# Turning half of a residual stream on TensorE instead of by VectorE and strip transfers, and spreading the strips that remain

## The chip, the core and the metric

The kernel runs on one core of a Trainium2 chip. It is a single launch; the metric is the device time of that launch in microseconds (us). The engines are TensorE (PE), VectorE (DVE), ScalarE (ACT), GpSimd (POOL) and SyncE (SP). In this kernel SP issues nearly all transfers, one after the other from one queue.

## What is computed

A trunk of two layers works on x of 256 rows and 2048 columns (float32), with 256 memory rows beside it. Each layer computes

```
h = rmsnorm(x, norm_g[l]);  proj = h @ w_in[l]              # 2048 x 7168
y_a = B * conv3(C * x_A) * silu(g_A)                        # 6 groups of 128 channels
y_d = headnorm(softmax(q1 k1) v - lam * softmax(q2 k2) v) * silu(g_D)   # 6 heads, q and k normed, distance bias
mkv = rmsnorm(mem, mem_norm_g[l]) @ w_mem_kv[l]             # 2048 x 1024
mk, mv = mkv[:, :512], mkv[:, 512:]                         # mk is normed per head of 128
y_m = softmax(mq mk) mv * silu(g_M)                         # 4 heads
x = x + concat(y_a, y_d, y_m) @ w_out[l]                    # 2048 x 2048
```

The memory keys mk and values mv of both layers depend on `mem` alone. The queries of the memory heads, and so the first use of mk, come late in a layer.

## The kernel before

**Blocks and chunks.** Every product with a weight matrix is cut into blocks of 512 output columns (`block`, line 264). A block has two accumulators (256 rows are two times 128) and goes over the 16 tiles of 128 rows of the weight. Two such tiles are a chunk: one load of 512 KB into `raw` (L249, four buffers), then ACT rounds it to `hi` and DVE takes the rest as `lo` (L259 and L260 with a gain for the memory weights, L255 and L256 for the others; four buffers each). Float32 is thus made of two rounded parts, and PE does three products for each of two row tiles and two weight tiles: `hi`, `lo` and once more `hi` against the stationary operand's two parts (L280 to L282). That is 12 matmuls of 128x512 per chunk and 8 chunks per block.

**Order of the work.** First the memory keys and values: layer 0's keys (chunks 0 to 7), layer 0's values (8 to 15), layer 1's keys (16 to 23), layer 1's values (24 to 31). Their stationary operand is `memT`, the transposed memory. From chunk 32 on layer 0 begins, whose first six blocks (32 to 79) give the queries, keys, values and a gate of the differential attention; the stationary operand is `xT`, x transposed and scaled by `norm_g`, as a pair of rounded parts. Then come the blocks of the memory heads' queries and gate, those of the convolution, and the output product, whose stationary operand is `yT`. Layer 1 does the same.

**Two ways of transposing.** One is on PE: `rows_T` (L568) has PE transpose tiles of 128x128 into PSUM, four of them (two column tiles by two row tiles) into one of two `pt` buffers, and ACT and DVE split the result into `xT` (`split_T`, L238 and L239, or L235 and L236 without a gain). `x_rows` (L577) does so for a list of column tiles, one group of four per step. The other way leaves PE alone: `turn_sheet` (L379) has DVE transpose the 32x32 blocks of a quarter, 512 columns by 256 rows, into a "sheet" (L386 from x, L383 in place), and then 16 transfers between parts of SBUF, called strips (L396, 32 KB each for a full sheet), move the blocks to their places. `x_turned` (L582) does so for a quarter of x, then splits it two column tiles at a time. The queries and keys of each layer, the memory keys and queries, and the operands of the convolution go by strips too.

**Planner.** After each chunk of a block the function `run_side` (L195) is called: it counts the chunk, issues up to `at_once[0]` strips from a queue `shifts`, steps every job in `tasks` whose due chunk has come, and steps one job in `side`. `later(job, n)` makes a job due n chunks from now. A job from `turn_sheet` first has DVE do its transposes, waits four or five chunks, puts its 16 strips into the queue and goes on when the last has been issued. `at_once` is 7 until layer 0's first block is done and 5 from then on. The strips stand on SP between the weight loads; while SP issues one it issues nothing else.

**The work that the change touches.** During layer 1's key block `x_load` (L644) loads x, two column tiles (256 KB) per chunk, into the buffer `xs`, which held `mem` before. After every second such load a quarter of x is complete, and an `x_turned` job is put into `tasks`: four quarters, with the buffers `v`, `ga`, `mga` and `mqT`, which are free until layer 0 needs them under those names. All 64 strips go into `shifts`. The memory keys are normed (`normed`, L341) into a sheet and turned by the job `keys` (L639), layer 0's from chunk 19 on, layer 1's from chunk 36 on; both sheets come from the two buffers of `e`, which the sheets of x use too (L585, L637, L663). At the end ACT scales them (L642).

The program's instructions are put into an order for each engine ahead of time; those marked by `keep_in_program_order`, the strips among them, stay in the order of the program among themselves. A queue or engine then works through its list strictly in order.

Of the kernel before, what the change touches and what calls it, by code (L numbers as in the profile page):

```python
# [18 lines left out]
P = 128  # L19
# [4 lines left out]
KT = D_MODEL // P  # L24
# [8 lines left out]
NB = 512  # L33
# [12 lines left out]
def encoder(ctx: ExitStack, tc: tile.TileContext, x, mem, norm_g, w_in, conv_w, conv_b,  # L46
# [20 lines left out]
    def nm(s):  # L67
        uid[0] += 1
        return f"{s}_{uid[0]}"
# [52 lines left out]
    def g_norm(l, k):  # L122
        return cvb[:, 64 + l * KT + k:65 + l * KT + k]
# [33 lines left out]
    def rsqrt(t, n):  # L157

        y = small.tile([P, n], F32, tag=f"rs_y{n}", name=nm("rsy"))
        a = small.tile([P, n], F32, tag=f"rs_a{n}", name=nm("rsa"))  # L160
        yi = y.bitcast(I32)
        nc.vector.tensor_scalar(yi, t.bitcast(I32), 1, None, ALU.logical_shift_right)
        nc.vector.tensor_scalar(yi, yi, -1.0, float(0x5F3759DF), ALU.mult, ALU.add)
        for _ in range(3):
            nc.vector.scalar_tensor_tensor(a, y, -0.5, y, ALU.mult, ALU.mult)
            nc.vector.tensor_tensor(a, a, t, ALU.mult)
            nc.vector.scalar_tensor_tensor(y, a, 1.5, y, ALU.add, ALU.mult)
        return y
# [2 lines left out]


    side, tasks, shifts = deque(), [], deque()
    at_once = [7]
    due = {}
    chunk = [0]

    def later(g, n):
        due[id(g)] = chunk[0] + n
        return g  # L180
# [157 lines left out]
    def col(st, which, t):  # L338
        return st[:, which, t:t + 1]

    def normed(acc, gs, st, home):  # L341

        ng = NB // gs
        ss = small.tile([P, NT, ng], F32, tag=f"ss{ng}", name=nm("ss"))
        for t in range(NT):
            sq = tmp.tile([P, NB], F32, tag="nat", name=nm("sq"), bufs=4)
            nc.scalar.activation(sq, acc[t], AF.Square)
            nc.vector.tensor_reduce(ss[:, t], sq.rearrange("p (g d) -> p g d", d=gs), AX.X, ALU.add)
            nc.vector.tensor_scalar(ss[:, t], ss[:, t], col(st, R2_64 if gs == HALF else R2_128, t), EPS,
                                    ALU.mult, ALU.add)  # L350
        r = rsqrt(ss.rearrange("p t g -> p (t g)"), NT * ng).rearrange("p (t g) -> p t g", t=NT)
        both = home()
        for t in range(NT):
            nc.vector.tensor_scalar(r[:, t], r[:, t], col(st, R, t), None, ALU.mult)
            w = min(gs // B, NA)
            nc.vector.tensor_tensor(
                both[:, :, :, t].rearrange("p (g b) j c -> p j g b c", b=w),
                acc[t].rearrange("p (j g b c) -> p j g b c", g=NA // w, b=w, c=B),
                r[:, t].rearrange("p (j g) -> p j g", g=NA // w).unsqueeze(3).unsqueeze(4)
                .to_broadcast([P, NB // P, NA // w, w, B]), ALU.mult)  # L360
        return both
# [4 lines left out]
    def sheet(home, tag, n=NB // P):  # L366
        return home.tile([P, NA, n, NT, B], F32, tag=tag, name=nm("sh"))

    def sheets(tag):
        return lambda: sheet(tmp if tag == "e" else keep, tag)  # L370
# [197 lines left out]
    def rows_T(dst, src, k, gain=None, n=2):  # L568

        pt = ps_t.tile([P, 2, SEQ], F32, tag="t", name=nm("pt"))  # L570
        for j in range(n):
            for t in range(NT):
                nc.tensor.transpose(pt[:, j, t * P:(t + 1) * P], src(k + j, t), ident)  # L573
        for j in range(n):
            split_T(dst, k + j, pt[:, j, :], None if gain is None else gain(k + j))

    def x_rows(dst, l, ks):  # L577
        for k in ks:
            rows_T(dst, lambda k, t: xs[:, t, k * P:(k + 1) * P], k, lambda k: g_norm(l, k))
            yield  # L580

    def x_turned(dst, l, b, tag, **how):  # L582

        whole = keep.tile([P, NB // P, SEQ], F32, tag=tag, name=nm("xf"))
        yield from turn_sheet(whole, sheet(tmp, "e"),  # L585
                              of=xs[:, :, b * NB:(b + 1) * NB], **how)
        for j in range(NB // P):
            k = b * NB // P + j
            pinned[0] = True
            split_T(dst, k, whole[:, j], g_norm(l, k))  # L590
            pinned[0] = False
            if j % 2:
                yield

    def stats_of(parts, tag):
        ss = small.tile([P, NT], F32, tag="ssum", name=nm("ssum"))
        nc.vector.tensor_reduce(ss, parts, AX.X, ALU.add)
        return row_stats(ss, tag)

    def T_tile(what):  # L600
        kept.append(big.tile([P, 2, KT, SEQ], F32R, tag="T", name=nm(what)))
        return kept[-1]
# [20 lines left out]
    def mem_square(k):  # L623

        load_constants((1, 2, 0, None)[k // 2] if k < 8 else None)
        if k == 8:
            rest_of_constants()
        if k < 8:
            c = k // 2
            for t in range(NT):  # L630
                sq = tmp.tile([P, NB], F32, tag="nat", name=nm("sq"), bufs=4)
                tc.keep_in_program_order(
                    nc.scalar.activation(sq, xs[:, t, c * NB:(c + 1) * NB], AF.Square, accum_out=ssm[:, t, c:c + 1]))

        if k == 10:
            stm.append(stats_of(ssm, "stm"))
            tasks.append(later(keys(0, normed(acc_k, P, stm[0], sheets("e"))), 6))  # L637

    def keys(l, nat):  # L639

        yield from turn_sheet(mkT[l], nat)
        tc.keep_in_program_order(nc.scalar.activation(mkT[l], mkT[l], AF.Copy, scale=mgain[:, l:l + 1]))  # L642

    def x_load(k):  # L644
        tc.keep_in_program_order(
            nc.sync.dma_start(xs[:, :, k * P:(k + 2) * P],
                              x[:, k * P:(k + 2) * P].rearrange("(t p) c -> p t c", p=P)))
        b, half = divmod(k + 2, NB // P)
        if not half:
            tasks.append(later(x_turned(xT, 0, b - 1, ("v", "ga", "mga", "mqT")[b - 1], wait=4), 1))  # L650

    mkT, mv, stm = [], [], []
    for l in range(DEPTH):
        if l > 0:
            xT = T_tile("xT")
        mkT.append(keep.tile([P, MH, SEQ], F32, tag=f"mkT{l}", name=f"mkT{l}"))
        mv.append(keep.tile([P, NT, W_MEM], F32, tag=f"mv{l}", name=f"mv{l}"))
        gm = lambda k: g_mnorm(l, k)
        pinned[0] = l == 0
        acc_k = block(memT, w_mem_kv[l], [(0, NB)], ALLK, gain=gm, before=mem_piece if l == 0 else x_load)  # L660
        pinned[0] = False
        if l > 0:
            tasks.append(later(keys(l, normed(acc_k, P, stm[0], sheets("e"))), 12))  # L663
        acc = block(memT, w_mem_kv[l], [(W_MEM, NB)], ALLK, gain=gm, before=mem_square if l == 0 else None,
                    )
        for t in range(NT):
            nc.scalar.activation(mv[l][:, t, :], acc[t], AF.Copy, scale=col(stm[0], R, t))
# [4 lines left out]
    for l in range(DEPTH):  # L672
# [4 lines left out]
        k2 = keep.tile([P, 2, DH - 4, SEQ], F32R, tag="bgT", name=nm("k2"))  # L677
        for b in range(6):
            acc = block(xT, w_in[l], [(C_D + b * NB, NB)], ALLK)
            at_once[0] = 5  # L680
            if b == 3:
                v = keep.tile([P, NT, W_DIFF], F32, tag="v", name=nm("v"))
                ga = keep.tile([P, NT, W_DIFF], F32, tag="ga", name=nm("ga"))
            if b < 3:
                tasks.append(later(qk_T(l, yT, k2, normed(acc, HALF, st, sheets("e")),
                                 (0, 0, 4) if b == 0 else (0, 4, 2) if b == 1 else None,
                                 (256, 0, 2) if b == 1 else (0, 2, 4) if b == 2 else None,
                                 ("mqT", "mga", "bgx")[b]), 8))
            else:
                for t in range(NT):  # L690
                    if b == 3:
                        nc.scalar.activation(v[:, t, 0:NB], acc[t], AF.Copy, scale=col(st, R, t))
                    elif b == 4:
                        nc.scalar.activation(v[:, t, NB:768], acc[t][:, 0:256], AF.Copy, scale=col(st, R, t))
                        silu2(ga[:, t, 0:256], acc[t][:, 256:512], st, t)
                    else:
                        silu2(ga[:, t, 256:768], acc[t], st, t)
# [4 lines left out]
        mqT = keep.tile([P, MH, SEQ], F32, tag="mqT", name=nm("mqT"))  # L702
        mga = keep.tile([P, NT, W_MEM], F32, tag="mga", name=nm("mga"))
# [91 lines left out]
        if l + 1 < DEPTH:  # L795
            xT = T_tile("xT")
# [53 lines left out]
```

## Time and profile before

| | |
|---|---|
| time, median of 3 runs | 965.05 us (965.03 to 965.42) |
| the profiled execution: its time, its span | 964.53 us, 962.7 us |
| busy PE, share of the span | 943.5 us, 98% |
| busy DVE, ACT | 647.5 us (67%), 509.0 us (53%) |
| mean granted TensorE clock | 0.993 |
| moved by DMA, mean rate | 187.30 MB, 195 GB/s |

Busy times of the engines overlap. PE's busy time is modelled: matmuls are pipelined, and one that runs at a lower clock counts as busy for longer. The second part of the page cuts the span into 40 slices and gives each engine's busy share in tenths, with the clock that PE was granted. The waits say who waited for whom. In a timeline each row has a start, a duration, the engine, the line, and in brackets the idle time just before it with what ended it; `SPq` rows are transfers being issued by SP. In an operation, `hi<-raw` means that `hi` was written from `raw`. Names of buffers: `raw`, `hi`, `lo` weights; `sh` a sheet; `xf`, `qk`, `mkT` what strips write; `pt` transposes on PE.

### The profile page before, as it was taken

The numbers are of one execution on the slowest core, as the hardware profiler recorded it, in microseconds if no ns is written. First come the engines' busy times: TensorE is split into PE (matmuls) and PEld (weight loads), VectorE is DVE, ScalarE is ACT, GpSimd is POOL, SyncE is SP. The second block draws the span as 40 slices with busy tenths as digits, with TensorE's granted clock in tenths as the row PEclk, the third lists the DMA queues.
The fourth block names the chain that finished last, engine by engine and source line by source line (L and its number), as shares of the span: only waits on it lengthen the run. The fifth ranks groups of instructions, "written<-read, shape, count | busy, mean of one in ns | idle before, by whom it ended". The sixth has DMA issues, their size and how long they took to land.

```text
span 962.7 us, 12648 instructions
## 1 busy us (share of the span) xinstructions
PE 943.5 (98%) x4298; PEld 777.1 (81%) x4298; DVE 647.5 (67%) x1188; ACT 509.0 (53%) x797; POOL 1.4 (0%) x8
## 2 busy tenths in 40 slices
PE   9997699999999999999999999999999999999998
PEld 6885478888888888888888888888888888888886
DVE  5776467866678875645775687855797766456753
ACT  5845455567456554444555544575555555435431
POOL 0000000000000000000000000000000000000000
PEclk9998999999999999999999999999999999999999
DMA  8766688776666555676677877776557556766862
GB/s 265 257 210 152 133 246 245 219 208 203 193 175 172 158 175 161 173 208 188 210 213 202 223 217 216 219 202 195 172 165 186 158 158 178 196 197 170 260 219 84
DMA packets 204133, 187.30 MB, mean 195 GB/s; under 512 B 106926, under 2 KB 130340, under 8 KB 204068
## 3 DMA queue, kind: packets, MB, share of 16 engines
q1 hardware_dynamic: 202724, 185.17, 66.7%
q10 hardware_dynamic: 1344, 1.33, 0.5%
q8 instruction: 33, 0.54, 0.2%
q14 instruction: 32, 0.26, 0.1%
HBM read 172.29 MB, written 2.10 MB: 181 GB/s over the span
## 4 chain that ended last, share of the span: by engine, by line
PE 94%; DMA 2%; SPq 2%; ACT 1%; DVE 0%; issue 0%; DVEq 0%; ACTq 0%
PE acc L282 29%; PE acc L281 29%; PE acc L280 29%; PE po L431 2%; SPq L396 1%; PE ptT L424 1%; DMA raw<-in_w_mem_kv_dram 1%; PE s L543 1%; PE s L493 1%; PE s L492 1%; PE pt L573 1%; ACT sq L608 1%; DMA raw<-in_w_in_dram 0%; PE py L416 0%; DMA xs<-in_mem_dram 0%; ACT hi L259 0%
## 5 line engine op out<-in xcount | busy, mean ns | idle before, releaser
L256 DVE TENSOR_TENSOR lo<-raw,hi 128x1024 fp32r<-128x1024 f32 x288 | 351.7, 1224 | 216.7 <-ACT hi L255 214.0
L255 ACT CAST hi<-raw 128x1024 fp32r<-128x1024 f32 x288 | 302.3, 1051 | 331.8 <-PE acc L282 271.8
L280 PE MATMUL acc<-hi,xT 128*128 128x512 f32 x896 | 352.9, 396 | 2.4 <-ACT hi L255 2.4
L281 PE MATMUL acc<-lo,xT 128*128 128x512 f32 x896 | 351.5, 392 | 1.0 <-DVE lo L256 1.0
L282 PE MATMUL acc<-hi,xT 128*128 128x512 f32 x896 | 351.3, 392 | 0.0
L280 PEld LDWEIGHTS acc<-hi,xT 128*128 128x128 f32 x896 | 168.4, 188 | 36.9 <-ACT hi L255 3.3
L281 PEld LDWEIGHTS acc<-lo,xT 128*128 128x128 f32 x896 | 168.8, 188 | 35.4 <-DVE lo L256 1.9
L282 PEld LDWEIGHTS acc<-hi,xT 128*128 128x128 f32 x896 | 168.7, 188 | 34.5
L281 PE MATMUL acc<-lo,yT 128*128 128x512 f32 x256 | 99.6, 389 | 0.0
L282 PE MATMUL acc<-hi,yT 128*128 128x512 f32 x256 | 99.6, 389 | 0.0
L280 PE MATMUL acc<-hi,yT 128*128 128x512 f32 x256 | 99.1, 389 | 0.0
L259 ACT ACTIVATE hi<-raw,cva 128x512 fp32r<-128x512 f32 x64 | 42.4, 716 | 35.1 <-DMA raw<-in_w_mem_kv_dram 24.4
L260 DVE SCALAR_TENSOR_TENSOR lo<-raw,cva,hi 128x512 fp32r<-128x512 f32 x64 | 45.5, 746 | 15.9 <-ACT hi L259 15.8
L281 PEld LDWEIGHTS acc<-lo,yT 128*128 128x128 f32 x256 | 48.1, 188 | 10.0
L280 PEld LDWEIGHTS acc<-hi,yT 128*128 128x128 f32 x256 | 48.1, 188 | 9.9
L282 PEld LDWEIGHTS acc<-hi,yT 128*128 128x128 f32 x256 | 48.1, 188 | 9.9
L281 PE MATMUL acc<-lo,memT 128*128 128x512 f32 x124 | 51.0, 412 | 2.6 <-DVE lo L260 2.5
L280 PE MATMUL acc<-hi,memT 128*128 128x512 f32 x124 | 43.4, 410 | 7.7 <-ACT hi L259 7.6
L282 PE MATMUL acc<-hi,memT 128*128 128x512 f32 x124 | 50.1, 404 | 0.0
L280 PEld LDWEIGHTS acc<-hi,memT 128*128 128x128 f32 x124 | 23.4, 195 | 14.4 <-ACT hi L259 9.3
L281 PEld LDWEIGHTS acc<-lo,memT 128*128 128x128 f32 x124 | 24.6, 198 | 10.2 <-DVE lo L260 5.1
L282 PEld LDWEIGHTS acc<-hi,memT 128*128 128x128 f32 x124 | 24.4, 197 | 5.1
(147 smaller groups left out, 652.6 us busy)
## 6 DMA issues: line engine op xcount, KB each, us to landing
raw<-in_w_in_dram SPq DMA_DIRECT2D x192, 512.0 KB
raw<-in_w_out_dram SPq DMA_DIRECT2D x64, 512.0 KB
raw<-in_w_in_dram SPq DMA_DIRECT2D x64, 256.0 KB
raw<-in_w_mem_kv_dram SPq DMA_DIRECT2D x31, 512.0 KB
xf<-sh SPq DMA_DIRECT2D x112, 32.0 KB
qk<-sh SPq DMA_DIRECT2D x96, 32.0 KB
xs<-in_x_dram SPq DMA_DIRECT2D x8, 256.0 KB
xs<-in_mem_dram SPq DMA_DIRECT2D x7, 256.0 KB
```

The source lines that it names most:

```text
L255: nc.scalar.copy(hi, raw)
L256: nc.vector.tensor_tensor(lo_, raw, hi.bitcast(F32), ALU.subtract)
L259: in_order(nc.scalar.activation(hi[:, j], raw[:, j], AF.Copy, scale=gains_of(j)), nc.vector.scalar_tensor_tensor(lo_[:, j], raw[:, j], gai ...
L260: nc.vector.scalar_tensor_tensor(lo_[:, j], raw[:, j], gains_of(j), hi[:, j].bitcast(F32), ALU.mult, ALU.subtract))
L280: nc.tensor.matmul(acc[t], sh, hi, start=first, stop=False)
L281: nc.tensor.matmul(acc[t], sh, lo, start=False, stop=False)
L282: nc.tensor.matmul(acc[t], sl, hi, start=False, stop=last)
L396: tc.keep_in_program_order(nc.sync.dma_start(d, s))
L424: nc.tensor.transpose(pt[:, k, i * P:(i + 1) * P], e[:, i, k * P:(k + 1) * P], ident)
L431: nc.tensor.matmul(po[:, i, :], eT[:, k, i * P:(i + 1) * P], v[:, k, h * P:(h + 1) * P], start=k == 0, stop=k == NT - 1)
L492: nc.tensor.matmul(s[c][:, i, :], qi, k_first(yT, c, h), start=True, stop=False)
L493: nc.tensor.matmul(s[c][:, i, :], qi, k_second(yT, k2, c, h), start=False, stop=True)
```

## The change

In the first part of the kernel x is now loaded from the middle: `x_load` takes column tiles 8 to 15 first and then 0 to 7. Only the last two quarters (columns 1024 to 2047) become `x_turned` jobs, with the buffers `mga` and `mqT`. The first two quarters become a job of `x_rows` in `side`, appended after layer 1's key block, so its four groups of transposes are stepped one per chunk from chunk 25 on. Until the end of layer 0's first block at most 3 strips go per chunk in place of 7, and from then on 4 in place of 5. Layer 0's memory keys are normed where they were, but into a sheet in buffer `v`, and their job is due 23 chunks later in place of 6, so at chunk 36; layer 1's use buffer `ga` and are due 14 later in place of 12, at chunk 38. Their strips follow five chunks after. Layer 1's x is turned as before, three quarters by strips and one on PE, with 4 strips per chunk.

```diff
-    at_once = [7]
+    at_once = [3]
...
-            tasks.append(later(keys(0, normed(acc_k, P, stm[0], sheets("e"))), 6))
+            tasks.append(later(keys(0, normed(acc_k, P, stm[0], sheets("v"))), 23))
...
     def x_load(k):
+        k = (k + KT // 2) % KT
         tc.keep_in_program_order(
             nc.sync.dma_start(xs[:, :, k * P:(k + 2) * P],
                               x[:, k * P:(k + 2) * P].rearrange("(t p) c -> p t c", p=P)))
-        b, half = divmod(k + 2, NB // P)
-        if not half:
-            tasks.append(later(x_turned(xT, 0, b - 1, ("v", "ga", "mga", "mqT")[b - 1], wait=4), 1))
+        b, more = divmod(k + 2, NB // P)
+        if not more and b > 2:
+            tasks.append(later(x_turned(xT, 0, b - 1, ("mga", "mqT")[b - 3], wait=4), 1))
...
         if l > 0:
-            tasks.append(later(keys(l, normed(acc_k, P, stm[0], sheets("e"))), 12))
+            tasks.append(later(keys(l, normed(acc_k, P, stm[0], sheets("ga"))), 14))
+            side.append(x_rows(xT, 0, range(0, KT // 2, 2)))
...
             acc = block(xT, w_in[l], [(C_D + b * NB, NB)], ALLK)
-            at_once[0] = 5
+            at_once[0] = 4
```

## Prediction

> **What bounds the kernel now.** I read the page first, then the PE waits, the queue of SP and the PE timeline of the one stretch that stands out.
>
> ```profile
> span 962.7 us, 12648 instructions
> ...
> PE   9997699999999999999999999999999999999998
> ...
> PEclk9998999999999999999999999999999999999999
> ```
>
> Each digit is a slice of 24.07 us. PE is full in nearly all of them, so time can be won only where it isn't: in the fourth and fifth slice (72 to 120 us), where the clock row has its one dip too. The waits give the amounts (in total, times, longest), over the whole span:
>
> ```profile
> engine line waited for: us in total, times, longest us
> PE acc L280 <- ACT hi L259: 7.6, 4, 2.5
> PE acc L281 <- DVE lo L260: 2.5, 3, 1.5
> PE acc L280 <- ACT hi L255: 2.4, 2, 2.0
> PE warm L114 <- DVE zeros L109: 1.2, 1, 1.2
> PE acc L281 <- DVE lo L256: 1.0, 2, 0.5
> PE pt L573 <- DMA xs<-in_mem_dram: 0.7, 1, 0.7
> ```
>
> Asked for 60 to 130 us alone, the view has the four rows of `acc` again with the same amounts, 13.5 us together; the other two (1.2 and 0.7) are the kernel's first microseconds, so after 130 us PE waits for nothing. Above them stands this row:
>
> ```profile
> ACT hi L259 <- DMA raw<-in_w_mem_kv_dram: 23.5, 7, 6.9
> ```
>
> ACT is not slow there, it waits for the weights `raw`. Why they come late is seen in the queue of SP, which issues weights and strips (start, us, what, how many); the last three rows are from layer 0:
>
> ```profile
> 61.08 4.66 SPq L396 DMA_DIRECT2D xf<-sh  x7
> ...
> 66.43 4.51 SPq L396 DMA_DIRECT2D xf<-sh  x7
> 71.04 0.55 SPq L249 DMA_DIRECT2D raw<-in_w_mem_kv_dram  x1
> ...
> 93.14 4.53 SPq L396 DMA_DIRECT2D xf<-sh  x7
> 97.77 0.55 SPq L249 DMA_DIRECT2D raw<-in_w_mem_kv_dram  x1
> ...
> 118.58 0.55 SPq L249 DMA_DIRECT2D raw<-in_w_in_dram  x1
> ...
> 166.86 0.55 SPq L249 DMA_DIRECT2D raw<-in_w_in_dram  x1
> 167.45 3.21 SPq L396 DMA_DIRECT2D qk<-sh  x5
> 170.75 0.55 SPq L249 DMA_DIRECT2D raw<-in_w_in_dram  x1
> ```
>
> Between two weight loads stand seven strips without a pause: 4.53 / 7 = 0.647 us each. One round is 0.59 (load, with the pause behind it, 166.86 to 167.45) + 4.53 + 0.10 (gap before the next) = 5.22 us, and the nine rounds from 71.04 to 118.58 take 47.54, 5.28 us each. SP is issue-bound. What PE wants is in its timeline:
>
> ```profile
> 59.83 0.39 PE L280 MATMUL acc<-hi,memT 128*128 128x512 f32 x1
> ...
> 62.55 0.39 PE L280 MATMUL acc<-hi,memT 128*128 128x512 f32 x1
> ...
> 77.50 0.62 PE L280 MATMUL acc<-hi,memT 128*128 128x512 f32 x2
> ...
> 84.84 0.39 PE L282 MATMUL acc<-hi,memT 128*128 128x512 f32 x1
> 87.30 0.73 PE L280 MATMUL acc<-hi,memT 128*128 128x512 f32 x2 [2.07 <-ACT hi L259]
> 89.53 0.80 PE L281 MATMUL acc<-lo,memT 128*128 128x512 f32 x1 [1.49 <-DVE lo L260]
> ...
> 97.42 0.61 PE L280 MATMUL acc<-hi,memT 128*128 128x512 f32 x2
> ...
> 127.96 0.61 PE L280 MATMUL acc<-hi,xT 128*128 128x512 f32 x2
> ```
>
> A chunk of weights is 12 matmuls, and at full pace 12 of them take 62.55 - 59.83 = 2.72 us (0.227 each). I number chunks from 0 at the kernel's start; 8 make a block. Chunk 24 (layer 1's memory values) starts at 77.50 and chunk 34 (layer 0's third) at 127.96: ten chunks in 50.46 us instead of 27.2. **Lost: 23.26 us**, of which 13.5 are waits and the rest, 9.8, is matmuls at a lower clock (the dip in the clock row). That is what the change is about; before and after the stretch PE is the bound.
>
> **What the change does, part by part.**
>
> *Fewer strips in the stretch.* Before, four quarters of x and layer 0's memory keys are in the queue together: 5 x 16 = 80 strips from chunk 23 on, at 7 per chunk, so until chunk 34. Afterwards it is two quarters, 32 strips; at 3 per chunk they end at chunk 33, but a round of SP is 3 x 0.647 + 0.59 + 0.10 = 2.63 us, under the 2.72 of PE. SP thus doesn't lose ground any more. It starts with a lead: chunk 24's load, which PE took up without a wait at 77.50, went out at 71.04 behind 14 strips; afterwards six stand there, so it goes 8 x 0.647 = 5.2 us earlier, and the lead then grows by about 0.1 per chunk. All of the 23.26 us should go. (At four a round would be 3.28: the smaller number per chunk is needed as well as the smaller total.) Bounds: 13.5 (only the waits) to 23.3 us; I take the upper end because the waits and the low clock have one start in the trace, chunk 25, and one end, chunk 33.
>
> *Transposes on PE.* Added are 4 groups (one per chunk, from chunk 25 on) of four 128x128 transposes. PE is full, so all of them count. The same group is in the first stage:
>
> ```profile
> 15.21 0.60 PE L573 MATMUL pt<-ident,xs 128*128 128x128 f32 x4
> ...
> 21.61 0.60 PE L573 MATMUL pt<-ident,xs 128*128 128x128 f32 x4
> ```
>
> A chunk with a group takes 3.20 us (21.61 - 15.21, halved), so a group costs 3.20 - 2.72 = 0.48 us, and four cost **1.9 us**. Bounds: nothing, if they fell into gaps; 4 x 0.60 = 2.4, if a group's whole length counted. That x for these columns is there: its loads are issued with chunks 20 to 23, and SP runs ahead of PE by several chunks.
>
> *What DVE and ACT get.* Of DVE's eight block transposes of x (two per quarter) four go, and the keys' one moves out of the stretch; the splits of xT into hi and lo are as many as before, half of them now reading `pt`.
>
> ```profile
> L386 DVE STREAM_TRANSPOSE sh<-xs 128x512 f32<-128x512 f32 x7 | 4.6, 690 | 8.1 <-DMA mkT<-sh 6.4 <-DMA xf<-sh 1.7
> L383 DVE STREAM_TRANSPOSE sh<-sh 128x1024 f32<-128x1024 f32 x2 | 2.4, 1220 | 0.0
> ```
>
> ```profile
> L238 ACT ACTIVATE xT<-xf,cvb x28: 492/495/508, 76.3 to 548.5; 128x256 fp32r<-128x256 f32 x28
> L238 ACT ACTIVATE xT<-pt,cvb x4: 460/470/475, 549.8 to 555.0; 128x256 fp32r<-128x256 f32 x4
> ```
>
> ```profile
> 40.00:60.00 20.00, 19.90 (x88) 16.18 (x87) 16.62 (x57) 11.46 (x20) 0.00 (x0) 1.00 0.92 307
> 60.00:130.00 70.00, 56.43 (x208) 41.75 (x207) 40.85 (x92) 35.88 (x67) 0.00 (x0) 0.90 0.63 155
> ```
>
> Splits from `pt` are no dearer (470 against 495 ns). The windows' columns are busy PE, weight load, DVE, ACT, POOL, then the clock and the DMA share. Shortened by the 21.3 of the sum below, the 70 us become 48.7; DVE's 40.85 less 3 x 0.69 + 1.22 = 3.3 (of the seven transposes in this window four stay) gives 37.6 us, 77%; ACT's 35.88 gives 74%. From 40 to 60 us DVE was at 83% with PE full. So neither is the next bound on the mean; what would be late next is a conversion held up by a burst (a rival). DVE's wait of 6.4 us for a sheet's free buffer goes too, because the keys no longer take the x sheets' buffers; it hides under SP's delay, and I count nothing.
>
> *Keys later.* 16 + 16 key strips now go with chunks 42 to 49, one sheet after the other, at 4 a chunk: 4 x 0.647 + 0.59 + 0.10 = 3.28 us against 2.72, so SP falls behind by 8 x 0.56 = 4.5 us. Behind these strips on SP stand the weights of layer 0, and PE would wait for those. Cover: layer 0's own strips go at five a chunk, in rounds of 170.75 - 166.86 = 3.89 us, so SP is 3 x 1.17 = 3.5 us behind after three of them, and PE has no wait there; and from chunk 34 to 41 SP has no strips and can fill its buffers. Price taken: 0; without that cover 4.5. On DVE and ACT two sheets pass where one did, about 1.2 us each, covered by the same slack. Memory heads read the keys only many chunks later. From 5 to 4 per chunk everywhere else: 16 strips take four chunks either way (5+5+5+1, 4+4+4+4); 0, and I see no gain either, as PE waits for nothing there.
>
> **Sum.** -23.26 + 1.9 = -21.3 us. The profiled execution took 964.53 (span 962.7), 0.52 under the median; from it comes 943.2, and from the median of 965.05 **943.7 us**.
>
> **The rivals.** *A burst makes conversions late.* PE's order is fixed: a third group of transposes waits until the two splits of the first have emptied one of two `pt` buffers, and those splits stand on ACT and DVE among weight conversions, the square sums of x, and layer 1's keys. The price of one such lateness is on the PE timeline: chunk 25 ends at 84.84 + 0.23 = 85.07, two chunks later it is 97.42 instead of 90.51, so 6.9 us, 3.56 of them waits and the rest the lower clock. One: 943.7 + 6.9 = 950.6; two: 957.5; three: 964.4, no change; **four, one for each group: 971.3, slower**. The tipping point is 21.3 / 6.9, just over three: it takes splits more than two chunks late each time. Against it: the means above, and layer 1's four splits from `pt` (last in the row quoted) belong to the same groups, without a wait of PE anywhere after 130 us. For it: by the code, layer 1's keys, the four groups' splits and those of the first quarter turned by strips all fall to DVE and ACT in chunks 24 to 29.
>
> *The transfers, not the issue, set the rounds.* A round carries 512 + 7 x 32 = 736 KB in 5.22 us; with three strips 608 KB, 4.31 us at the same rate, so 9 x 0.91 = 8.2 us are won and 1.9 paid: 958.7. Against it: SP never pauses between strips, the DMA share is 0.63 there and 0.92 from 40 to 60 us, at twice the rate. The Trainium skill speaks for this rival ("DMA: Bandwidth & Descriptors", section "Issuing engines are not separate DMA queues"): it holds the sequencer's time to initiate a transfer to be usually small beside the transfer. By that rule the sum would be this rival's; the trace disagrees, with 0.647 us of issue per strip and the engines more than a third idle.
>
> *The low clock has a cause of its own and stays.* Then only the 13.5 us of waits are won: 965.05 - 13.5 + 1.9 = 953.5. Against it: the clock row dips in the slices with the waits and nowhere else, and the 3.35 us beyond the waits of 87.30 and 89.53 are lost right behind them. The Trainium skill ("TensorE: Matmul & The Clock Gate", section "What's actually happening") has the clock halve after an idle window of about 3.4 us; no single wait here is longer than 2.5. By that rule these gaps would not slow the clock, and something else would; the trace agrees with it that slow stretches follow idleness, not on the length that is needed.
>
> **How the numbers follow.** Chances: forecast 0.74; one late burst 0.12, two 0.03, three 0.02, four 0.03; transfers 0.04; clock 0.02. Low end: transposes at nothing, 965.05 - 23.26 = 941.8, and 0.3 for the spread of runs: 941.5. High end: one late burst, 950.6, and 2.4 more, about the longest single wait of PE: 953. That holds 0.86 by this count; it isn't made narrower, as its terms come from one execution. About 0.2% (1.9 us) is what a measurement can tell from no change: faster by more 0.95, within 0.02 (three bursts), slower 0.03 (four).
>
> **What would show it.** Right: slices 4 and 5 of PE at 9, the clock at 1.00 throughout from 60 us on, rounds on SP of one load and three strips with SP pausing for buffers, ten chunks from 24 in 27.2 + 1.9 = 29.1 us, the strips into `xf` down from 112 to 80 in all, transposes into `pt` up by 16, and key strips between layer 0's weights four at a time. Wrong: PE waits for `hi` or `lo` between chunks 24 and 34 (burst), SP pausing while ACT waits for `raw` (transfers), a lower clock without waits, or new PE waits after chunk 42, where the keys' strips now are.

## The result, and the profile after

The changed kernel takes 942.99 us (median of 4 runs, 942.94 to 943.25), the kernel before 965.23 (4 runs, 965.03 to 965.68): a ratio of 0.9769 with a 95% interval of 0.9753 to 0.9786. 943.7 was forecast. The profiled execution took 942.94, its span is 940.6, 22.1 under that of before.

The page of the changed kernel, slices of 23.5 us:

```profile
span 940.6 us, 12637 instructions
...
PE   9999999999999999999999999999999999999998
...
PEclk9999999999999999999999999999999999999999
```

The dip of PE and that of the clock are gone. The waits of PE over the whole span are down to two rows, both of the kernel's first microseconds:

```profile
PE warm L114 <- DVE zeros L109: 1.2, 1, 1.2
PE pt L573 <- DMA xs<-in_mem_dram: 1.1, 2, 0.8
```

The queue of SP in the stretch, and (last three rows) where the keys' strips now are:

```profile
55.42 2.42 SPq L396 DMA_DIRECT2D xf<-sh  x3
...
63.86 0.37 SPq L249 DMA_DIRECT2D raw<-in_w_mem_kv_dram  x1
...
66.27 0.55 SPq L249 DMA_DIRECT2D raw<-in_w_mem_kv_dram  x1
66.86 1.89 SPq L396 DMA_DIRECT2D xf<-sh  x3
68.85 0.55 SPq L249 DMA_DIRECT2D raw<-in_w_mem_kv_dram  x1
...
85.11 0.55 SPq L249 DMA_DIRECT2D raw<-in_w_in_dram  x1
...
111.46 0.55 SPq L249 DMA_DIRECT2D raw<-in_w_in_dram  x1
112.06 2.55 SPq L396 DMA_DIRECT2D mkT<-sh  x4
114.70 0.55 SPq L249 DMA_DIRECT2D raw<-in_w_in_dram  x1
```

A round of three is 68.85 - 66.27 = 2.58 us, one of four 3.24. Note the first row: strips begin at 55.42, where they began at 61.08 before. That turns out to matter below. The PE timeline, from the last matmul of chunk 15 to the first of chunk 32 and two chunks on:

```profile
54.68 0.39 PE L282 MATMUL acc<-hi,memT 128*128 128x512 f32 x1
54.91 0.60 PE L573 MATMUL pt<-ident,xs 128*128 128x128 f32 x4
...
66.71 0.49 PE L573 MATMUL pt<-ident,xs 128*128 128x128 f32 x3
...
77.50 0.39 PE L280 MATMUL acc<-hi,memT 128*128 128x512 f32 x1
...
82.94 0.27 PE L573 MATMUL pt<-ident,xs 128*128 128x128 f32 x1
...
85.81 0.60 PE L573 MATMUL pt<-ident,xs 128*128 128x128 f32 x4
...
98.75 0.60 PE L573 MATMUL pt<-ident,xs 128*128 128x128 f32 x4
...
100.35 0.39 PE L280 MATMUL acc<-hi,xT 128*128 128x512 f32 x1
...
105.81 0.39 PE L280 MATMUL acc<-hi,xT 128*128 128x512 f32 x1
```

Chunk 15 ends at 54.68 + 0.23 = 54.91. Sixteen chunks of 2.72 us end at 98.43, and chunk 32 begins at 100.35: 1.92 us for the four groups of transposes (the second of them with one transpose apart, at 82.94). Chunk 24 begins at 77.50, as before. Chunk 34 begins at about 105.8 where it was 127.96: 22.15 us, the whole difference of the spans. The window of the stretch, shortened by the forecast's 21.3 us (busy PE, weight load, DVE, ACT, POOL, clock, DMA share, GB/s):

```profile
60.00:108.70 48.70, 48.70 (x222) 40.24 (x221) 39.17 (x92) 34.72 (x65) 0.00 (x0) 1.00 0.77 213
```

DVE is at 80% and ACT at 71% (77 and 74% in the prediction), and PE waits for neither.

### The profile page after: what moved, and what is told of

Same layout as the page of the kernel before. It is cut to its first block, busy times and chain, and to the rows that moved or that the text cites. A ratio compares the mean times of both kernels' runs of the same rounds, so it can differ in the third digit from the quotient of the medians.

```text
span 940.6 us, 12637 instructions
## 1 busy us (share of the span) xinstructions
PE 934.6 (99%) x4314; PEld 774.6 (82%) x4314; DVE 645.1 (69%) x1184; ACT 508.9 (54%) x797; POOL 1.4 (0%) x8
## 4 chain that ended last, share of the span: by engine, by line
PE 98%; DMA 1%; SPq 0%; issue 0%; DVE 0%; DVEq 0%
PE acc L282 31%; PE acc L280 31%; PE acc L281 31%; PE po L431 2%; PE ptT L424 1%; DMA xs<-in_mem_dram 1%; PE s L543 1%; PE s L493 1%; PE s L492 1%; PE pt L573 1%; PE py L416 0%; SPq L619 0%; SPq L249 0%; DVE xs L810 0%; DVEq L847 0%
## 5 line engine op out<-in xcount | busy, mean ns | idle before, releaser
L281 PE MATMUL acc<-lo,memT 128*128 128x512 f32 x124 | 48.5, 391 | 0.0
```

The source lines that it names most:

```text
L281: nc.tensor.matmul(acc[t], sh, lo, start=False, stop=False)
```

## The experiments

**Theories.** *Issue*: the rounds are set by the time SP needs to issue a strip. Rivals: *transfer* (the bytes set them), and, inside the issue theory, which of the three parts does the work: fewer strips in all, fewer per chunk, or the keys moved. Each time is compared with that of the kernel before, measured beside it: 964.58 us for the first four kernels below, 963.90 for the keys alone and the last two kernels, 964.65 for the others.

**A strip with a quarter of its bytes** (kernel before).

```diff
+        if chunk[0] < 40:
+            nc.gpsimd.memset(dst[:, 1:], 0.0)
...
+                if chunk[0] < 40:
+                    s, d = s[:, 0:1], d[:, 0:1]
```

> The kernel before, with each of the 80 strips between chunks 23 and 34 carrying one column tile in place of four (8 KB for 32 KB; the other three tiles of xT's and the layer-0 keys' buffers are cleared by POOL instead, so this part of the result is left out). The count of strips and all their places on SP stay. Issue theory (a strip costs SP its 0.65 us whatever it carries): rounds stay at 5.2 us, time 963 to 966. Transfer theory (the bytes set the round): a round of 568 KB in place of 736 takes 4.0 us, nine of them win about 11 us, time 953 to 955.

Measured: 962.43 us, 0.997 of before (0.9958 to 0.9981). SP in this kernel, then the window 60 to 130 us:

```profile
91.69 0.53 SPq L249 DMA_DIRECT2D raw<-in_w_mem_kv_dram  x1
92.27 4.47 SPq L400 DMA_DIRECT2D xf<-sh  x7
96.83 0.53 SPq L249 DMA_DIRECT2D raw<-in_w_mem_kv_dram  x1
```

```profile
60.00:130.00 70.00, 57.62 (x213) 41.85 (x212) 41.63 (x93) 36.79 (x67) 0.00 (x0) 0.93 0.44 134
```

The DMA share fell from 0.63 to 0.44, and seven strips still take 4.47 us, a round 5.14. The 2 us won are far from the 11 that bytes would give; where they come from is not shown. The Trainium skill ("DMA: Bandwidth & Descriptors", section "Issuing engines are not separate DMA queues") expects the initiating time to be usually small beside the transfer; here, at 0.64 us for 8 KB, it is what counts.

**The same strips from POOL's queue** (kernel before).

```diff
-                tc.keep_in_program_order(nc.sync.dma_start(d, s))
+                tc.keep_in_program_order((nc.gpsimd if chunk[0] < 40 else nc.sync).dma_start(d, s))
```

> The kernel before, with all strips up to chunk 40 issued by POOL in place of SP; nothing else. Issue theory: SP has only weight loads there, its rounds fall under 2.72 us and PE does not wait for weights between chunks 24 and 32. If POOL issues a strip in under 0.68 us, the last quarter of x is there in time for chunk 38 and the time is 965.2 - 23.3 = 942; at 1 us a strip the 80 strips end at 61 + 80 = 141 us, some 25 us after PE wants the last quarter, and the loss comes back as a wait for xT in place of one for weights. Transfer theory: the same bytes over the same engines, rounds of 5.2 us, 965.

Measured: 959.13 us, 0.9944 (0.9929 to 0.9959). The waits of PE:

```profile
PE acc L280 <- DVE sh L356: 4.4, 1, 4.4
PE acc L280 <- ACT xT L238: 3.1, 2, 1.5
PE acc L282 <- DVE xT L239: 2.5, 2, 1.2
...
PE acc L281 <- DVE lo L256: 0.5, 1, 0.5
```

PE no longer waits for `hi` of any weight, as the issue theory has it, and for `lo` 0.5 us in the stretch; the transfer theory would have kept 965. New waits take most of it back: for `xT`, whose strips are late, and 4.4 us for accumulators that a norm (L356) still holds. That norm is not one of the memory keys, whose last is at 115.78, but that of layer 0's first block:

```profile
145.96 1.28 ACT L347 ACTIVATE sq<-acc 128x512 f32<-128x512 f32 x2 [0.98 <-PE acc L282]
...
151.40 1.28 ACT L347 ACTIVATE sq<-acc 128x512 f32<-128x512 f32 x2 [0.98 <-PE acc L282]
```

```profile
155.57 1.28 DVE L356 TENSOR_TENSOR sh<-acc,rsy 128x512 f32<-128x512 f32 x2
```

The norm's squares (L347) follow the ends of layer 0's first two blocks, 5.44 us apart where a block takes 21.76: 5.44 us are the two chunks that need the last quarter of x, which ACT splits at 137.16 only. So the first block ended late, and the third (at 156.40) had to wait for its accumulators. POOL's queue shows where the strips lose time:

```profile
84.12 9.21 POOL L396 DMA_DIRECT2D xf<-sh  x16 [1.59 <-DMA mkT<-sh]
99.98 7.16 POOL L396 DMA_DIRECT2D xf<-sh  x12 [6.65 <-DVE sh L386]
```

A strip costs POOL 0.58 us, fast enough, but its queue stands for 6.65 us at one time until DVE has transposed the next quarter. By the program six sheets share two buffers; that this made the quarter late is likely, not shown.

**The halving alone** (kernel before, x from the middle, first half on PE; 7 strips per chunk, keys early).

```diff
+        k = (k + KT // 2) % KT
...
+        if not more and b > 2:
+            tasks.append(later(x_turned(xT, 0, b - 1, ("mga", "mqT")[b - 3], wait=4), 1))
...
+            side.append(x_rows(xT, 0, range(0, KT // 2, 2)))
```

> The kernel before with only the halving: x loaded from the middle, its first half turned by PE, its second by strips; still 7 strips per chunk, and the memory keys early, as before. Issue theory: 48 strips are 6.9 rounds of 5.2 us, 17 us behind PE; less the lead that SP had in the kernel before (there 11.4 rounds were 28.6 us behind and 23.3 were lost, so a lead of 5 us), 12 us are lost and 1.9 paid for the transposes: 954 to 957. If the total number of strips were all that counts (48 of 80): 14 us lost and 1.9 paid, 957 to 958. If the halving alone did it: 943.

Measured: 952.84 us, 0.9881 (0.9866 to 0.9896), 11.7 us won with the transposes paid. It is better than expected by 1 to 4 us; why is not shown, as the strips begin at 61.10 us, like before. PE still waits for weights:

```profile
PE acc L280 <- ACT hi L259: 4.0, 3, 1.8
PE acc L281 <- DVE lo L260: 2.4, 1, 2.4
```

**The changed kernel at 7 strips per chunk.**

```diff
-    at_once = [3]
+    at_once = [7]
```

> The changed kernel with 7 strips per chunk until the end of layer 0's first block, in place of 3; keys late and half of x on PE, as changed. Issue theory: 32 strips are 4.6 rounds of 5.2 us, 11.4 us behind, less a lead of 5 us: 6.4 lost, 948 to 950. If the smaller number per chunk counts for nothing: 943.

Measured: 944.85 us, 0.9795 (0.9780 to 0.9809), 19.7 us won. The expected 5 to 7 us of loss against the changed kernel did not come: of PE's waits only this one is in the stretch,

```profile
PE acc L281 <- DVE lo L260: 0.2, 1, 0.2
```

so with 32 strips the rate hardly matters. The lead of SP was larger than I had it: here the strips begin at 55.97.

**The keys alone** (kernel before, sheets of their own, late; 64 strips at 7 per chunk).

```diff
-            tasks.append(later(keys(0, normed(acc_k, P, stm[0], sheets("e"))), 6))
+            tasks.append(later(keys(0, normed(acc_k, P, stm[0], sheets("bgx"))), 23))
...
-            tasks.append(later(keys(l, normed(acc_k, P, stm[0], sheets("e"))), 12))
+            tasks.append(later(keys(l, normed(acc_k, P, stm[0], sheets("bgT"))), 14))
```

> The kernel before with only the memory keys moved: normed into sheets of their own (buffers of later stages that are free then) and turned from chunks 36 and 38 on; all four quarters of x by strips, still 7 per chunk. Count theory (only the strips between the weight loads count): 64 strips in place of 80 are 2.3 rounds less, 2.5 us each: 5.7 us won, 959. Start theory (the keys' sheet also held up the first transposes of x, so strips began at 61.1 us in the kernel before and at 55.4 in the changed one): some 4 to 5 us more, 954 to 955.

Measured: 955.03 us (954.47 to 958.28), 0.9915 (0.9893 to 0.9937): 8.9 us, more than 16 strips can explain by their count.

**The keys' buffers alone**, the turn as early as before (`sheets("bgx")` with 6, `sheets("bgT")` with 12).

> The kernel before with only other buffers for the sheets of the memory keys: those of their own that the run with the late keys had, but turned as early as before. All 80 strips at 7 per chunk stay. Start theory in its buffer form (keys and x take sheets from one pair of buffers in the order of the program, so x's first transposes stood behind the keys'): strips start near 55.5 us in place of 61, 4 to 5 us won, 959 to 961. If it was the early turn of the keys that held x up and not the shared pair: no change, 964 to 965.

Measured: 960.43 us, 0.9958 (0.9941 to 0.9975), 4.2 us won with all 80 strips at 7 per chunk. SP's first strips in this kernel:

```profile
54.92 0.37 SPq L249 DMA_DIRECT2D raw<-in_w_mem_kv_dram  x1
55.35 4.67 SPq L396 DMA_DIRECT2D xf<-sh  x7
```

Why they were later is on DVE. First the kernel before, then this one:

```profile
58.55 0.69 DVE L356 TENSOR_TENSOR sh<-acc,rsy 128x512 f32<-128x512 f32 x1
59.16 0.70 DVE L386 STREAM_TRANSPOSE sh<-xs 128x512 f32<-128x512 f32 x1
```

```profile
51.73 1.30 DVE L386 STREAM_TRANSPOSE sh<-xs 128x512 f32<-128x512 f32 x2
...
60.41 1.28 DVE L356 TENSOR_TENSOR sh<-acc,rsy 128x512 f32<-128x512 f32 x2
```

That the buffers hold x up, and not the early turn of the keys, is what this run shows. How they do is read from the program: one pair of buffers is handed out in its order, the keys' sheet first, so x's first transpose stood behind the keys' norm (L356). With other buffers it runs 7 us earlier (at 51.83 in the changed kernel), and SP issues strips in time in which it used to wait.

**The smaller number alone** (kernel before, `at_once = [3]`).

> The kernel before with only the smaller number: 3 strips per chunk until the end of layer 0's first block, still 80 strips with the keys early. Issue theory: PE no longer waits for weights up to chunk 33, but at 3 per chunk only some 30 of 80 strips are out when layer 0 begins; at its second or third chunk the missing quarter is forced, and all the strips that are left, about 47, go at once: 30 us in which SP issues no weights, less a lead of some 8: 22 lost in place of 23, so 962 to 970, no real gain. If the smaller number is what counts: 942 to 945.

Measured: 967.09 us, 1.0024 (1.0015 to 1.0034): slower. SP, and what PE waited for:

```profile
95.86 0.37 SPq L249 DMA_DIRECT2D raw<-in_w_in_dram  x1
96.28 28.73 SPq L396 DMA_DIRECT2D xf<-sh  x44
125.11 8.97 SPq L249 DMA_DIRECT2D raw<-in_w_in_dram  x5
```

```profile
PE acc L280 <- ACT xT L238: 21.3, 1, 21.3
```

Weights come in time until x is needed, and then 44 strips go in one piece.

**The changed kernel again**, as the measure for the three kernels that follow.

> The changed kernel once more, so that the other kernels of this call can be set against it on the same chip: 943 to 944 if before is 965.

> The changed kernel again, as the measure for the other kernels of this call: 943 to 944.

Measured: 943.50 us (ratio 0.9782, 0.9768 to 0.9797), beside the last two kernels, and 943.08 us (0.9777, 0.9763 to 0.9792), beside the one that comes next.

**Each group of transposes twice** (changed kernel).

```diff
-            rows_T(dst, lambda k, t: xs[:, t, k * P:(k + 1) * P], k, lambda k: g_norm(l, k))
+            for _ in range(2 if l == 0 else 1):
+                rows_T(dst, lambda k, t: xs[:, t, k * P:(k + 1) * P], k, lambda k: g_norm(l, k))
```

> The changed kernel with layer 0's four groups of transposes on PE made twice, each with its splits (the second result overwrites the first with the same values). If a group costs what the first stage showed (0.48 us of a full PE): 1.9 us more than the changed kernel, 945 to 946. If a group falls into gaps: no difference. If the splits hold up PE: one late burst of the prediction, 6.9 us more, 950.

Measured: 945.45 us (945.27 to 945.88) against 943.08: 2.4 for four more groups, about 0.6 each (2.9 by the two profiles, less their first 15 us). One of its waits is for the additional splits (0.2 us, ACT xT L238).

**One quarter on PE, three by strips.**

```diff
-        k = (k + KT // 2) % KT
+        k = (k + KT // 4) % KT
...
+        if not more and b > 1:
+            tasks.append(later(x_turned(xT, 0, b - 1, ("mga", "mqT", "bgx")[b - 2], wait=4), (1, 1, 6)[b - 2]))
...
-            side.append(x_rows(xT, 0, range(0, KT // 2, 2)))
+            side.append(x_rows(xT, 0, range(0, KT // 4, 2)))
```

> A version between the two: one quarter of x on PE, three by strips at 3 per chunk, the third of them turned five chunks later so that a sheet is free; the rest as in the changed kernel. Issue theory: rounds of 2.63 us still keep up with PE, two groups of transposes fewer win 0.96 us, 942 where the changed kernel has 943; the last strips go with chunk 38, where the last quarter is first used, so a wait of PE for xT there is what it risks: each 2.5 us of it is one late burst as in the prediction, 949.

Measured: 942.22 us (942.00 to 942.61), ratio 0.9771 (0.9757 to 0.9786), against 943.50 and 0.9782 (0.9768 to 0.9797) for the changed kernel beside it. The runs do not overlap, the intervals do. It has no wait for weights; one of 0.3 us is new (ACT mv L669). Of the 1.0 us between the two profiles 0.7 is in the first 15 us, which this version does not touch. That it is better is likely, and not settled.

**No quarter on PE, strips by POOL**, the keys late and in sheets of their own as in their run above, and 4 strips per chunk in place of 5 after layer 0's first block.

> No quarter of x on PE: all four by strips, issued by POOL up to chunk 40, 7 per chunk; the keys in sheets of their own and late, by SP at 4 per chunk. If what POOL's strips lost in the first such run (10.5 us of PE waits for xT and for the keys' accumulators) came from six sheets sharing two buffers, it goes: all four groups of transposes are saved, 941. If four sheets in two buffers are still late for chunks 32 to 38: 945 to 950.

Measured: 944.75 us, 0.9798 (0.9784 to 0.9813). Two waits are left where the first POOL run had three:

```profile
PE acc L280 <- ACT xT L238: 1.5, 1, 1.5
...
PE acc L280 <- ACT sq L347: 0.6, 1, 0.6
```

The wait for the norm is gone, and of xT's most, though POOL's queue still stands for 6.14 us at one time. What remains costs more than the transposes saved: 1.25 us slower than the changed kernel beside it (943.50).

## Why the prediction was right, and where it was not

*SP is issue-bound in the stretch: right.* A quarter of the bytes changed a round from 5.22 to 5.14 us, and without strips on SP the waits for weights were gone but for 0.5 us.

*All of the 23.26 us come back, waits and low clock together: right.* No wait of `acc` and no dip of the clock is left. The rivals of the transfers and of a clock with a cause of its own fall with it, and no burst made conversions late.

*The transposes cost 1.9 us: right*, 1.92 on the PE timeline; four more groups cost 2.4. Where they would stand was wrong: not one per chunk from chunk 25 on, but far apart, in chunks 16, 20, 27 and 31 (54.91, 66.71, 85.81 and 98.75 us). So the ten chunks from 24 on took 28.31 us and not 29.1. Since PE is full, that changed nothing in the sum.

*The smaller number per chunk is needed as well: wrong.* It was worked out from rounds of 3.28 us at four, without asking how far SP's lead carries. At seven the changed kernel loses hardly anything: the profiles are 942.0 and 941.2 us long (the latter of the repeat, whose first 15 us match). Alone the smaller number makes it 0.24% slower. My own lead of 5 us, used for the expectations of two experiments, was too small: in the changed kernel at seven for the same reason as the next step, in the halving alone for one that stays open.

*The wait of 6.4 us for a sheet's buffer counts at nothing: the step that failed.* The row quoted for it, at 75 us, was indeed hidden; but the same pair of buffers also set when the first strips could begin, and that sat on the path. Giving the keys other buffers, and nothing else, starts the strips at 55.35 instead of 61.08 us and wins 4.2 us. I had put that part of the gain down to the round length. The lead was mis-sized with it: chunk 24's load went out at 63.86 instead of 71.04, 7.2 us earlier and not 5.2. The sum held because its term was the whole loss, whatever removed it; in this the number was lucky. Whether all of it would have come back without the earlier start was not run.

How the 20 to 22 us divide: the halving alone 11.7, the keys alone 8.9 (other buffers for them, without more, 4.2), the two with the later rate of four 19.7. 11.7 + 8.9 = 20.6, so they nearly add up; the smaller number in the first part is worth about 0.8 more, by the profiles above.

*Keys later cost nothing: right.* PE has no wait after its first microseconds, in rounds of 3.24 us (3.28 forecast). *SP would pause for buffers: hardly*; it issued nothing from 60.96 to 63.86, but from there to 85.11 it issues almost without a gap, at a pace just above that of PE.

*The remaining 0.8 us* (22.1 of span against 21.3): about 0.4 was lost before chunk 24 already (chunk 16 started 0.26 late, for one), which I had not counted, and 0.4 lies in the first 15 us. There three profiles of the same changed kernel differ by 0.7 us (a group of transposes at 14.74, 15.29 and 14.57; 15.21 in that of before), so this last part is no effect of the change.

## What to carry to other kernels

A queue that issues everything in order is a resource like an engine: count what it has to issue between two loads that the bound engine needs, at the measured time of issue, and compare with that engine's pace. Then ask when the queue could have begun, since a lead of some microseconds is spent or saved there: here a shared pair of buffers cost 4.2 us in a row that reads like idle time of another engine. Reducing the rate without the total only moves the heap to the point where the data are needed.

## What the runs showed of the hardware

Issue time barely depends on size: a strip of 32 KB took SP 0.647 us, one of 8 KB 0.64, a weight load of 512 KB 0.55 (0.37 in some rows). From POOL's queue a strip took 0.58 us (16 in 9.21). Three profiles of the same kernel differ by up to 0.7 us in their first 15 us.

The low clock is seen in the distance between matmuls. In the kernel before, right behind the waits of 2.07 and 1.49 us, they stand 0.43 us apart from 90.12 to 95.24 us, where 0.227 is the full pace:

```profile
90.12 0.63 PE L282 MATMUL acc<-hi,memT 128*128 128x512 f32 x1
90.55 0.63 PE L281 MATMUL acc<-lo,memT 128*128 128x512 f32 x1
```

Behind shorter ones, 1.08 and 0.47 us at chunk 25, they are back at 0.227 within about 1 us.
